# Softmax on one core: on exit Pool awaits the last stores, in place of SyncE

## The chip, the cores and the metric

One of the cores of a Trainium2 chip. The metric is device microseconds of one execution.

## The reference

```python
x = randn(16, 1024, 512), float32
x_max = np.max(x, axis=-1, keepdims=True)
exp_x = np.exp(x - x_max)
return exp_x / np.sum(exp_x, axis=-1, keepdims=True)
```

16384 rows of 512 elements: 33.6 MB in, 33.6 MB out.

## The kernel before

Loads are issued by SyncE (SP), stores by ScalarE (ACT). The framework ends a program with a block in which SyncE waits until every semaphore has its final value, all engines meet at a barrier that Pool (GpSimd) runs, Pool clears the semaphores, and a second barrier follows. The kernel edits that block when the program is complete, and has already merged the two barriers into one:

```python
def one_barrier_on_exit(nc):
    end = nc.main_func.blocks[2].instructions
    def of(engine, kind):
        return [i for i in end if i.engine == engine and type(i).__name__ == kind]
    for engine in (Activation, PE, DVE, SP):         # names shortened, an assertion cut
        arrivals = [i for i in of(engine, "InstDrain") if i.has_update()]
        leaves = of(engine, "InstEventSemaphore")
        end.remove(leaves[0])
        end.remove(arrivals[1])
    gather, release, gather_2, release_2 = of(Pool, "InstEventSemaphore")
    end.remove(release)
    end.remove(gather_2)
```

What is left in the exit block, engine by engine, as the built program has it (the compiler splits a drain's list of awaited semaphores into instructions of at most two semaphores, and leaves one with the drain):

```
SP    wait: store queue 3
SP    wait: store queues 4 and 2
SP    wait: store queues 5 and 1
SP    wait: queue 6 (the LAST store) and queue 0
SP    wait: queue 7 and VectorE's count
SP    drain, waits for ScalarE's count            } the moved drain
SP    drain, arrives at the barrier               (ACT, PE, DVE: likewise)
Pool  drain
Pool  gather: waits for four arrivals
Pool  drain ("reset drain"), clear of the semaphores, drain, release
all   leave when released
```

The first drain of the list is the "moved drain" of this document, Pool's wait for the four arrivals is the "gather", and the way from SyncE's arrival to Pool's gather is the "hop".

Of the kernel before, what the change touches and what calls it, by code (L numbers as in the profile page):

```python
# [1 line left out]

# [4 lines left out]

F32 = mybir.dt.float32
EXP = mybir.ActivationFunctionType.Exp
AX = mybir.AxisListType.X  # L10


CHUNKS = [
    (3, 0), (5, 3), (8, 8), (16, 16), (16, 32), (16, 48), (16, 64), (16, 80), (16, 0), (16, 16),
]
SBUF_ROWS = 96

EARLY = 8
AFTER_STORE = {2: [8], 3: [9]}

GROUP = 8

FINISH_BEFORE = (1, 2, 3)

STORE_ROWS = {3: 8, 4: 8, 5: 8}

ON_ACT = ()

AT_HEAD = {mybir.EngineType.SP: 3}



def loads_at_the_head(nc):

    main, body = nc.main_func.blocks[0], nc.main_func.blocks[1]
    for engine, count in AT_HEAD.items():
        loads = [
            i
            for i in body.instructions
            if i.engine == engine and type(i).__name__ == "InstDMACopy"  # L40
        ][:count]
        barrier = next(
            n
            for n, i in enumerate(main.instructions)
            if i.engine == engine and type(i).__name__ == "InstDrain"
        )
        for load in loads:
            body.instructions.remove(load)
        main.instructions[barrier:barrier] = loads
# [10 lines that stand above are left out]
    for engine in (  # L60
        mybir.EngineType.Activation,
        mybir.EngineType.PE,
        mybir.EngineType.DVE,
        mybir.EngineType.SP,
    ):
        arrivals = [i for i in of(engine, "InstDrain") if i.has_update()]
        leaves = of(engine, "InstEventSemaphore")
        assert len(arrivals) == len(leaves) == 2
        end.remove(leaves[0])
        end.remove(arrivals[1])  # L70
    gather, release, gather_2, release_2 = of(mybir.EngineType.Pool, "InstEventSemaphore")
    end.remove(release)
    end.remove(gather_2)

@with_exitstack
def kernel(
    ctx: ExitStack,
    tc: tile.TileContext,
    x: bass.AP,
    out: bass.AP,  # L80
):
    nc = tc.nc
    nc.at_finalize(loads_at_the_head)
    nc.at_finalize(one_barrier_on_exit)
    P = nc.NUM_PARTITIONS

    x_flat = x.flatten_outer_dims()
    out_flat = out.flatten_outer_dims()
    n, d = x_flat.shape
    assert n == P * sum(R for R, _ in CHUNKS)  # L90


    src, dst, at = [], [], 0
    for R, _ in CHUNKS:
        for flat, views in ((x_flat, src), (out_flat, dst)):
            part = flat[at : at + P * R, :]
            views.append(part.rearrange("(p r) d -> p r d", r=R))
        at += P * R

    data = ctx.enter_context(tc.tile_pool(name="data", bufs=1))  # L100
    stats = ctx.enter_context(tc.tile_pool(name="stats", bufs=4))
    held = data.tile([P, SBUF_ROWS, d], F32, name="held")
    place = [held[:, s : s + R, :] for R, s in CHUNKS]


    groups = []
    for k, (R, _) in enumerate(CHUNKS):
        m = -(-R // GROUP)
        cuts = [R * i // m for i in range(m + 1)]
        since = 0  # L110
        for a, b in zip(cuts, cuts[1:]):
            ends = b == R or b - since >= STORE_ROWS.get(k, R)
            groups.append((k, a, b, since if ends else None))
            since = b if ends else since
    shift = [None] * len(groups)
    sums = [None] * len(groups)

    def load(k):
        queue = nc.scalar if k in ON_ACT else nc.sync
        queue.dma_start(out=place[k], in_=src[k])  # L120

    def rowmax(g):
        k, a, b, _ = groups[g]
        shift[g] = stats.tile([P, b - a], F32, name="shift", tag="shift")
        nc.vector.reduce_max(  # L125
            out=shift[g], in_=place[k][:, a:b, :], axis=AX, negate=True
        )

    def exps(g):
        k, a, b, _ = groups[g]  # L130
        sums[g] = stats.tile([P, b - a], F32, name="sums", tag="sums")
        for r in range(a, b):
            nc.scalar.activation(  # L133
                out=place[k][:, r, :],
                in_=place[k][:, r, :],
                func=EXP,
                bias=shift[g][:, r - a : r - a + 1],
                scale=1.0,
                accum_out=sums[g][:, r - a : r - a + 1],
            )  # L140

    def scale(g):
        k, a, b, since = groups[g]
        recip = stats.tile([P, b - a], F32, name="recip", tag="recip")
        nc.vector.reciprocal(out=recip, in_=sums[g])  # L145
        for r in range(a, b):
            nc.vector.tensor_scalar_mul(  # L147
                out=place[k][:, r, :],
                in0=place[k][:, r, :],
                scalar1=recip[:, r - a : r - a + 1],  # L150
            )
        if since is not None:
            nc.scalar.dma_start(
                out=dst[k][:, since:b, :], in_=place[k][:, since:b, :]
            )
        if b == CHUNKS[k][0]:
            for later in AFTER_STORE.get(k, ()):
                load(later)

    with tc.manual_schedule():  # L160
        for k in range(EARLY):
            load(k)
        waiting = None
        for g, (k, a, _, _) in enumerate(groups):
            if waiting is not None and a == 0 and k in FINISH_BEFORE:
                scale(waiting)
                waiting = None
            rowmax(g)
            exps(g)
            if waiting is not None:  # L170
                scale(waiting)
            waiting = g
        scale(waiting)


# [1 line left out]
_INS = ['x']  # L177
_OUTS = [((16, 1024, 512), 'float32')]


# [23 lines left out]
```

## Time and profile before

| | before |
|---|---|
| median of the first three runs | 161.48 us (161.41 to 161.56) |
| span of the profiled run | 159.586 us |
| last store: issued, 16th increment of its semaphore | 144.932 us, 158.883 us |
| that landing to the end of the span | 703 ns |
| end of the span to the last semaphore update of the execution | 1941 ns |

The lines that carry this are in the prediction. Read the table as a sum of three terms: the landing (the moment of the 16th increment, 158.883 us), the handshake (from there to the end of the span, 703 ns), and the close (from there to the last semaphore update, 1941 ns). The measured time is a little less than the sum: this execution took 161.41 us, and the sum is 161.527. In all 13 profiles the time lies 0.105 to 0.120 us below the sum; why is not shown, but it is nearly constant, so a change of the sum shows in the time.

### The profile page before, as it was taken

What the parts mean: (1) busy time and instruction counts of PE and PEld (TensorE: products, weight loads), DVE (VectorE), ACT (ScalarE), POOL (GpSimd) and SP (SyncE); (2) the same over time, 40 slices, a digit from 0 to 9 for tenths busy, and PEclk for the clock granted to TensorE, in tenths of its full rate; (3) what the DMA queues carried; (4) which work ended last, traced back from release to release, by engine and by line L of the source; (5) the groups of instructions that cost most, each with busy time, mean ns of one, the idle gap of its engine ahead of it and who ended that gap; (6) DMA issues with size and microseconds to landing.
All of it is one profiled execution on the core that took longest, in us unless ns stands there. A gap on an engine that the chain in (4) does not pass through costs nothing.

```text
span 159.6 us, 511 instructions
## 1 busy us (share of the span) xinstructions
DVE 123.9 (78%) x162; ACT 93.3 (58%) x257; POOL 0.2 (0%) x4
## 2 busy tenths in 40 slices
DVE  0482880799699999999999999999999999853000
ACT  0717119207994959595958687776868595940000
POOL 0000000000000000000000000000000000000000
DMA  7999999899999999999899999999999999999993
GB/s 267 443 456 432 399 414 466 375 404 467 411 446 411 485 419 396 439 411 493 378 448 439 411 497 411 405 444 402 435 444 485 411 402 468 435 402 419 485 411 164
DMA packets 3315, 67.13 MB, mean 421 GB/s; under 512 B 368, under 2 KB 368, under 8 KB 624
## 3 DMA queue, kind: packets, MB, share of 16 engines
q1 hardware_dynamic: 1440, 33.56, 49.4%
q10 hardware_dynamic: 1872, 33.56, 49.0%
q14 instruction: 3, 0.02, 0.0%
HBM read 33.55 MB, written 33.55 MB: 421 GB/s over the span
## 4 chain that ended last, share of the span: by engine, by line
DVE 71%; ACT 14%; issue 3%; DMA 3%; DVEq 0%; ACTq 0%
DVE shift L125 39%; DVE held L147 30%; ACT held L133 14%; DMA held<-in_x_dram 3%; DVE recip L145 2%; DVEq L199 0%; ACTq L133 0%
## 5 line engine op out<-in xcount | busy, mean ns | idle before, releaser
L133 ACT ACTIVATE held<-held,shift 128x512 f32<-128x512 f32 x128 | 90.5, 708 | 43.4 <-DVE shift L125 33.3
L125 DVE TENSOR_REDUCE shift<-held 128x8 f32<-128x4096 f32 (+2 forms) x17 | 70.7, 4164 | 4.6 <-DMA held<-in_x_dram 4.6
L147 DVE TENSOR_SCALAR held<-held,recip 128x512 f32<-128x512 f32 x128 | 52.2, 482 | 0.6
L133 ACT ACTIVATION_READ_ACCUMULATOR held<-held,shift 128x1 f32 x128 | 23.9, 187 | 0.0
L145 DVE RECIPROCAL recip<-sums 128x8 f32<-128x8 f32 (+2 forms) x17 | 3.3, 195 | 15.8 <-ACT held L133 15.8
L133 ACT ACT_TABLE_LOAD x1 | 1.3, 1283 | 4.7 <-DMA held<-in_x_dram 4.7
L188 POOL MEMSET const-bfloat16-1.0<- 128x1 bf16 x1 | 0.1, 103 | 0.0
L188 POOL MEMSET const-uint8-127<- 128x1 uint8 x1 | 0.1, 102 | 0.0
L188 POOL MEMSET const-float32-1.0<- 128x1 f32 x1 | 0.1, 100 | 0.0
L188 POOL MEMSET const-float32-0.0<- 128x1 f32 x1 | 0.1, 99 | 0.2 <-issue 0.2
## 6 DMA issues: line engine op xcount, KB each, us to landing
held<-in_x_dram SPq DMA_DIRECT2D x7, 4096.0 KB, 41.8
out_dram<-held ACTq DMA_DIRECT2D x4, 4096.0 KB, 20.9
out_dram<-held ACTq DMA_DIRECT2D x7, 2048.0 KB, 35.3
held<-in_x_dram SPq DMA_DIRECT2D x1, 2048.0 KB, 11.7
held<-in_x_dram SPq DMA_DIRECT2D x1, 1280.0 KB, 7.2
out_dram<-held ACTq DMA_DIRECT2D x1, 1280.0 KB, 19.9
held<-in_x_dram SPq DMA_DIRECT2D x1, 768.0 KB, 4.6
out_dram<-held ACTq DMA_DIRECT2D x1, 768.0 KB, 15.6
```

The source lines that it names most:

```text
L125: nc.vector.reduce_max(out=shift[g], in_=place[k][:, a:b, :], axis=AX, negate=True)
L133: nc.scalar.activation(out=place[k][:, r, :], in_=place[k][:, r, :], func=EXP, bias=shift[g][:, r - a : r - a + 1], scale=1.0, accum_out=s ...
L145: nc.vector.reciprocal(out=recip, in_=sums[g])
L147: nc.vector.tensor_scalar_mul(out=place[k][:, r, :], in0=place[k][:, r, :], scalar1=recip[:, r - a : r - a + 1],)
L188: nc = _bacc.Bacc("TRN2", target_bir_lowering=False, num_devices=1)
```

## The change

The intent: SyncE waits for the stores and then only tells Pool so. If Pool waits itself, SyncE's arrival is early and the hop from one engine to the other leaves the end of the execution.

```diff
     end.remove(release)
     end.remove(gather_2)
+
+    done = of(mybir.EngineType.SP, "InstDrain")[0]
+    end.remove(done)
+    at = next(n for n, i in enumerate(end) if i.name == gather.name)
+    end.insert(
+        at,
+        mybir.InstDrain(
+            name=done.name, engine=mybir.EngineType.Pool,
+            ins=[], outs=[], sync_info=done.sync_info,
+        ),
+    )
```

More of the change, by code (lines that the diff above doesn't have):

```diff
@@ L73, in one_barrier_on_exit @@
     end.remove(gather_2)
+    done = of(mybir.EngineType.SP, "InstDrain")[0]
[4 more added lines that the diff above has]
+        mybir.InstDrain(
+            name=done.name,
+            engine=mybir.EngineType.Pool,
+            ins=[],
+            outs=[],
+            sync_info=done.sync_info,
+        ),
+    )
 @with_exitstack
```

## The prediction

> **What bounds the kernel now.** I read the page first, then cut the last 15 us into stretches, then asked the waits of SyncE's queue, then the instructions of the exit line in the last 0.8 us, and last the trace's records there one by one, because the page counts no drain or semaphore instruction as busy.
>
> From the page, the busy time of the engines, the DMA share over 40 slices of 4 us, and the two data queues (loads on q1, stores on q10):
>
> ```profile
> DVE 123.9 (78%) x162; ACT 93.3 (58%) x257; POOL 0.2 (0%) x4
> ...
> DMA  7999999899999999999899999999999999999993
> ...
> q1 hardware_dynamic: 1440, 33.56, 49.4%
> q10 hardware_dynamic: 1872, 33.56, 49.0%
> ```
>
> DMA is at 80% or more from the second slice to the last but one, and the two queues together fill 98.4% of the 16 engines' span. So transfers are the bound: 67.13 MB at the page's mean of 421 GB/s are 159.5 us of a 159.6 us span. GpSimd (Pool) does four memsets at the start and nothing else.
>
> The end, in stretches (columns: length, busy us of DVE, ACT and POOL with counts, clock, DMA share, GB/s):
>
> ```profile
> 145.00:150.00 5.00, 0.00 (x0) 0.00 (x0) 0.00 (x0) 1.00 1.00 433
> 150.00:155.00 5.00, 0.00 (x0) 0.00 (x0) 0.00 (x0) 1.00 1.08 465
> 155.00:159.60 4.60, 0.00 (x0) 0.00 (x0) 0.00 (x0) 1.00 0.43 185
> ```
>
> No engine computes after 145 us; the end is set by the stores draining, and after them by whatever handshake follows. The page's chain stops at the last VectorE multiply and says nothing of this end. The waits of SyncE's queue do:
>
> ```profile
> SPq L199 <- DMA out_dram<-held: 76.0, 4, 47.1
> SPq L199 <- PEq L199: 0.5, 1, 0.5
> ```
>
> SyncE has nothing left to issue after 82.8 us and sits in exit waits for stores (76.0 us in all), then 0.5 us for its own release. That release is put down to PE only because PE counts the same semaphore down; Pool raises it. The instructions of the exit line between 158.8 us and the end (count: shortest/median/longest ns, first and last start):
>
> ```profile
> L199 SPq EVENT_SEMAPHORE  x3: 17/27/28, 158.9 to 159.5; - x3
> L199 SPq DRAIN  x2: 7/7/7, 159.0 to 159.1; - x2
> L199 POOLq EVENT_SEMAPHORE  x2: 17/17/17, 159.1 to 159.5; - x2
> L199 POOLq DRAIN  x2: 34/52/70, 159.2 to 159.4; - x2
> L199 POOLq EVENT_SEMAPHORE_RANGE_CLEAR  x1: 93/93/93, 159.3 to 159.3; - x1
> ```
>
> All of it lies within 0.69 us. A drain takes 7 ns on SyncE, but 34 and 70 ns on Pool. The single records (start in ns, duration, instruction):
>
> ```
> 158883      -  the last store's semaphore gets its 16th increment
> 158900     27  SyncE waits: last store, and one older store
> 158961     28  SyncE waits: another store queue, and VectorE's count
> 159026      7  SyncE drain: ScalarE's count          <- moves to Pool
> 159085      7  SyncE drain: arrives at the barrier   <- stays on SyncE
> 159117     17  Pool waits for four arrivals
> 159198     70  Pool drain
> 159297     93  Pool clears the semaphores
> 159419     34  Pool drain
> 159482     17  Pool releases; the others leave at 159524 to 159535
> 159586         end of the span
> ```
>
> **What the Trainium skill says.** "Perfetto Trace Analysis", section "Sequencer-only Instruction (DRAIN, etc)", says that the profiler reports only the execution of such an instruction, not its wait nor the time for its update to spread. The trace agrees: SyncE's 7 ns drain is followed 59 ns later by the next instruction, so spacings have to be counted, not durations. "VectorE: DVE Perf Modes", section "The DRAIN you can't avoid", has boilerplate drains at about 12 ns on all five engines. For Pool this trace disagrees (34 and 70 ns here, 181 ns behind the memsets at the start), and the measurement decides. "DMA: Bandwidth & Descriptors", section "Why a DMA increments its semaphore by 16 and not by 1", says that the engines of one transfer finish independently and only the full 16 means landed. Here the 16 increments of the last store spread from 157.686 to 158.883 us, and SyncE moves on 17 ns after the sixteenth. "Runtime: NRT & Kernel Launch", section "The ~15µs preamble/postamble breakdown", has a barrier, a semaphore reset and more behind a kernel. The trace shows semaphore updates until 161.53 us, 1.9 us past the span, which accounts for 161.48 against 159.6. The change touches none of it.
>
> **The change, part by part.** It takes SyncE's first exit drain with its list of awaited semaphores and puts it on Pool, just before Pool waits for the four arrivals. In the built program the list becomes five semaphore instructions and the drain, in the old order, with the last store in the fourth of them. SyncE's arrival stays, but now comes at about 83 us instead of 159.085. Nothing in the loop, the loads or the stores moves. The order of instructions on each engine is otherwise the same but for line numbers.
>
> Removed from the path: SyncE's drain to its arrival, 59 ns, and the arrival to Pool's wake, 159117 - 159085 = 32 ns. Together 91 ns.
>
> Added to the path: Pool must run the same three instructions, then a fourth of its own, where it was standing ready before. Steps from the landing:
> - Landing to first wait passed: 17 ns on SyncE; no Pool wake from a DMA is in the trace, so I keep 17. Start at 158900.
> - First wait to second: 61 ns on SyncE (158900 to 158961). Pool's only two back-to-back semaphore instructions, in the entry barrier, are 78 ns apart (1525 to 1603), the first with an update that these lack. 61 to 78.
> - Second wait to drain: 65 ns on SyncE; on Pool 81 both at entry (1603 to 1684) and at exit (159117 to 159198), again with updates. 65 to 81.
> - Drain to the wait for arrivals: Pool's two exit drains lead to the next instruction after 99 ns (70 ns long) and 63 ns (34 ns long), so 29 ns plus the drain. 63 to 99.
>
> Sum 189 to 258 ns, so Pool's wait for arrivals would start at 159089 to 159158 against 159117 now. The arrivals are in by then (SyncE 83 us, VectorE and ScalarE by 145.5 us), so it passes at once. From there on all is the same. The change is worth between -28 ns and +41 ns; the middle is +7 ns, which is nothing: 0.004% of 161.48.
>
> **Rivals.** (1) The handshake disappears for its full 91 ns. It would need Pool to be as quick as SyncE, with a 7 ns drain, and a free final wait; 161.39 us. Against it are the two Pool drains above and the fact that the arrivals' wait still has to be executed. (2) Pool's drain is slow, as the 181 ns one behind the memsets, or Pool wakes slowly from a DMA's semaphore: 29 + 181 = 210 ns instead of 63 to 99 gives 161.6. Against it: that drain had memsets in flight, while at exit Pool has been idle for 158 us, and the drain at 1684 took 41 ns. (3) SyncE, freed at 83 us, lets something start earlier. But its last load is issued by then in both kernels, and ScalarE issues all stores, so there is nothing to start; no gain. (4) The whole exit handshake, 158883 to 159586 or 0.70 us, were saved: not on offer, and even that would be only 0.4%. Nothing in the trace carries this past 2%.
>
> **Range and chances.** The effect is smaller than the scatter of the three runs (161.41 to 161.56), so the prediction is the old median, 161.48. The range has to hold run scatter of 0.15 us, a possible different chip or session, which the trace does not tell, and rivals 1 and 2 (161.39 and 161.6). I take 161.25 to 161.70. A change of 2% would be 3.2 us, 4.6 times the whole handshake, so within 2% has 0.985; the rest is for what I do not see.
>
> **What would show it right or wrong.** In the changed profile the exit's store waits should appear on Pool's queue, SyncE's one wait there should be some 76 us for its release, and DMA rows and queue shares should be the same to 0.2 points. From the sixteenth increment of the last store to the end of the span it was 703 ns; I expect 675 to 744 ns. The moved drain should last 34 to 70 ns; 7 ns would speak for rival 1, over 150 ns for rival 2. I would be wrong if the landing-to-end interval changed by over 100 ns, or if the last store itself landed at another time by more than the scatter, which would mean that an idle Pool or SyncE queue touches the transfers.

## The result, and the profile after

The changed kernel took 161.53 us (median of 6 runs, 161.43 to 161.63), the kernel before 161.47 us (6 runs, 161.41 to 161.65). The ratio is 1.0002, with a 95% interval of 0.9989 to 1.0014: the same. Ratios here are the mean time of one kernel's fast runs over that of the other's of the same rounds, so not quite the ratio of the medians quoted.

Busy times and data queues of the page, changed kernel:

```profile
DVE 123.9 (78%) x162; ACT 93.3 (58%) x257; POOL 0.2 (0%) x4
...
q1 hardware_dynamic: 1440, 33.56, 49.5%
q10 hardware_dynamic: 1872, 33.56, 48.9%
```

The last stretches, changed kernel (length, busy DVE, ACT, POOL, clock, DMA share, GB/s):

```profile
145.00:150.00 5.00, 0.00 (x0) 0.00 (x0) 0.00 (x0) 1.00 0.99 426
150.00:155.00 5.00, 0.00 (x0) 0.00 (x0) 0.00 (x0) 1.00 1.05 452
155.00:159.81 4.81, 0.00 (x0) 0.00 (x0) 0.00 (x0) 1.00 0.46 198
```

Work and transfers are those of before: queue shares moved by 0.1 points, and the same bytes drain at the end. What moved is the wait. SyncE's own queue, changed kernel, first line of its waits:

```profile
SPq L214 <- PEq L214: 76.5, 1, 76.5
```

The 76.0 us of store waits are gone from SyncE; it now waits once for its release (again put down to PE, which counts the same semaphore down). The store waits are on Pool, under a line of the library, because the compiler made them from an instruction that carries no line of the kernel:

```profile
bacc.py:44 POOLq EVENT_SEMAPHORE  x5: 17/43/43, 130.1 to 159.2; - x5
```

And the exit line from 158.8 us on, changed kernel (shortest/median/longest ns, first and last start):

```profile
L214 POOLq EVENT_SEMAPHORE  x2: 17/17/17, 159.3 to 159.7; - x2
L214 POOLq DRAIN  x2: 34/52/70, 159.4 to 159.6; - x2
L214 POOLq EVENT_SEMAPHORE_RANGE_CLEAR  x1: 92/92/92, 159.5 to 159.5; - x1
L214 SPq EVENT_SEMAPHORE  x1: 17/17/17, 159.7 to 159.7; - x1
```

Two things are to be seen. A wait instruction for two semaphores takes 43 ns on Pool (median of the five), against 27 and 28 ns on SyncE before. And only two Pool drains are recorded where three ran: the moved one has no source line at all and is left out, which is why the page counts 510 instructions and before 511. Record by record, with the time since the landing:

```
ns after the landing of the last store       before          changed
wait: last store, queue 0                    SP    17        Pool  24
wait: queue 7, VectorE                       SP    78        Pool 111
drain: ScalarE                               SP   143        Pool (not recorded)
arrival                                      SP   202        (early)
Pool's gather                                     234             276
reset drain                                       315             357
clear                                             414             456
last drain                                        536             578
release                                           599             641
end of the span                                   703             745
```

From gather to end it is 469 ns in both. Ahead of it the changed kernel needs 276 ns where the old one needed 234: the hop is gone with the step to it, and what came in its place costs 42 ns more.

The landing itself was at 159.061 us in this profile and at 158.883 us before, 178 ns later, which is most of the difference of the two spans. Whether the change did that had to be tested.

### The profile page after: what moved, and what is told of

Its sections match the earlier page's. It is cut to its first block, busy times and chain, and to the rows that moved or that the text cites. A ratio compares the mean times of both kernels' runs of the same rounds, so it can differ in the third digit from the quotient of the medians.

```text
span 159.8 us, 510 instructions
## 1 busy us (share of the span) xinstructions
DVE 123.9 (78%) x162; ACT 93.3 (58%) x257; POOL 0.2 (0%) x4
## 4 chain that ended last, share of the span: by engine, by line
DVE 70%; ACT 14%; issue 3%; DMA 3%; DVEq 0%; ACTq 0%
DVE shift L140 38%; DVE held L162 30%; ACT held L148 14%; DMA held<-in_x_dram 3%; DVE recip L160 2%; DVEq L214 0%; ACTq L148 0%
```

## The experiments

**The theory:** every sequencer instruction behind the last landing is on the path with its start-to-start spacing, and these spacings are longer on Pool than on SyncE; that gives back the hop. **The rivals:** the waiting engine moves the landing; the handshake is absorbed by what follows the kernel; Pool's drain alone is to blame; Pool wakes slowly.

All edits stand behind the two removals at the end of `one_barrier_on_exit` of the kernel before. `made(...)` only builds an instruction and gives it the source line of `gather`, so that it is recorded. `waits` is the list of the SyncE drain `done`, `place_of(...)` finds an instruction's place in the block, `Event` is a semaphore instruction and `Drain` a drain. The diffs are cut to the lines that make the difference. "Spacing" is the time from the start of one instruction to the start of the next on its engine.

### The changed kernel with its drain made visible

```diff
+    end.remove(done)
+    end.insert(place_of(gather), made(Drain, done.name, POOL, waits))
```

> The changed kernel with only a source line given to the moved drain, so that the trace records it. My theory (Pool runs the same wait instructions more slowly, and that gives the saved hop back): from the landing of the last store's 16th increment to the end of the span 745 ns, within 10 of the first profile of the changed kernel (before: 703); Pool's wait starts 24 ns after the landing, the next 87 ns later, the drain 80 to 90 ns after that, lasts 34 to 70 ns, and the wait for arrivals follows after 75 to 85 ns. Rival (the 178 ns later landing in the first profile of the changed kernel is caused by Pool waiting in place of SyncE): the last store lands near 159.06 us again and the times lie 0.1 to 0.2 us above before in all rounds. My theory: the times of both kernels share the same range, 161.4 to 161.65.

Measured: 161.54 us (5 runs, 161.44 to 161.72; before 161.46, ratio 1.0007, interval 0.9995 to 1.0020). Landing to end 745 ns again. The exit line from 158.8 us on:

```profile
L215 POOLq EVENT_SEMAPHORE  x4: 17/30/43, 159.1 to 159.7; - x4
L215 POOLq DRAIN  x3: 34/34/70, 159.2 to 159.6; - x3
```

Now three drains are there. By records: wait at 24 ns after the landing, next wait 86 later, drain 87 later, lasting 34 ns, gather 78 later. These intervals are as the theory had them; the times are not quite (it had put both kernels at 161.4 to 161.65; the runs reach from 161.44 to 161.72, and from 161.32 to 161.59 before). The landing was at 159.053 us, which the rival of the moved landing had asked for too; the other runs have to decide that.

### Ten more satisfied waits, on Pool and on SyncE

```diff
+    old = [w for w in waits if w.ant_name.startswith(("DMAHW0", "DMAHW1"))]
+    for k in range(10):                       # Pool version, in the changed kernel
+        end.insert(place_of(gather), made(Event, f"I-{9000 + k}", POOL, old))
```

```diff
+    for k in range(10):                       # SyncE version, in the kernel before
+        end.insert(place_of(done) + 1, made(Event, f"I-{9000 + k}", SP, old))
```

> The changed kernel with ten more semaphore instructions on Pool behind the store waits, each of two semaphores long satisfied. My theory (each instruction behind the landing adds its spacing to the end, about 87 ns on Pool): landing to end 745 + 870 = 1615 ns, time 162.3 to 162.5. Rival (the handshake lies beside the close of the execution and is absorbed): landing to end longer in the trace, but time still 161.4 to 161.7.

> The kernel before with the same ten semaphore instructions on SyncE, between its store waits and its arrival. My theory: 61 ns each on SyncE, landing to end 703 + 610 = 1313 ns, time 162.0 to 162.2, so 26 ns less for each instruction than on Pool. Rival (the two engines are alike and the 42 ns are something else, such as a Pool wake or the drain): the ten cost the same on both, within 5 ns each.

Measured on Pool: 162.34 us (4 runs; ratio to before 1.0055, 1.0042 to 1.0069), landing to end 1612 ns. On SyncE: 162.09 us (4 runs; 1.0040, 1.0025 to 1.0056), landing to end 1313 ns. Exit line from 158.8 us on, Pool version, then SyncE version:

```profile
L218 POOLq EVENT_SEMAPHORE  x14: 17/43/43, 158.9 to 160.4; - x14
L218 POOLq DRAIN  x3: 34/34/70, 159.1 to 160.3; - x3
```

```profile
L216 SPq EVENT_SEMAPHORE  x13: 17/28/28, 159.0 to 160.2; - x13
L216 SPq DRAIN  x2: 7/7/7, 159.1 to 159.8; - x2
```

The same instruction, with semaphores that had long been satisfied, lasts 43 ns on Pool and 28 on SyncE. The ten add 867 ns on Pool (1612 - 745) and 610 ns on SyncE (1313 - 703), 26 ns more each on Pool. The times follow: the means lie 0.88 and 0.64 us above those of the kernel before, against 0.91 and 0.61 us in the trace. So nothing behind the kernel absorbs the handshake; that rival falls.

The Pool version holds one more finding. The compiler merged waits so that the first of the ten had one semaphore and the gather got two. The one with a single semaphore is followed by the next after 60 ns, all others after 86 or 87; the gather with two is followed by the reset drain after 107 ns, and with one after 80 or 81 in the other profiles in which the reset drain follows it directly. By these two comparisons the second semaphore of a wait costs 26 or 27 ns on Pool. Other pairs give somewhat less: 25 in the next experiment, and 20 or 21 in the two profiles of the reset version below, where a wait for one semaphore is followed after 66 ns.

### No drain among Pool's waits

```diff
-    end.insert(place_of(gather), made(Drain, done.name, POOL, waits))
+    end.insert(place_of(gather), made(Event, done.name, POOL, waits))
```

> The changed kernel with the moved drain replaced by a semaphore instruction; the waits are paired anew, with the last store in the third of five, so that as many instructions follow it as in the changed kernel. My theory (the number of Pool instructions counts, not that one is a drain): landing to end 735 to 765 ns, against 745. Rival (the Pool drain is the culprit): 40 ns or more shorter than 745.

The removed line is that of the version with the visible drain. Measured in one run of unknown state (161.52 us): landing to end 780 ns. That is 35 ns longer than with the drain, outside the 735 to 765 of my theory, and far from the rival's 705. By records, three spacings of 86, 87 and 87 ns lead from the first wait to the gather, and the gather, which got a second semaphore in the new pairing, is followed after 106 ns where it was 81. So nearly all of the excess is 25 ns for that second semaphore and 9 for a two-semaphore wait (87) in the drain's place (78). The moved drain is not what makes the changed kernel 42 ns longer: it is the cheapest of the three moved steps. But this run is no test of drain against wait alone, since the new wait has two semaphores and the drain had one. Where both have one, the drain is the dearer: it is followed after 78 or 79 ns, the wait after 60 (66 in the reset version).

### The last store awaited last, on SyncE and on Pool

```diff
+    waits.sort(key=lambda w: not w.ant_name.startswith("DMAHW6"))
+    end[place_of(done)] = made(Drain, done.name, SP, waits)          # SyncE version
```

```diff
+    waits.sort(key=lambda w: not w.ant_name.startswith("DMAHW6"))
+    end.remove(done)                                                 # Pool version
+    end.insert(place_of(gather), made(Drain, done.name, POOL, waits))
```

> The kernel before with SyncE's list of waits in another order: the last store is now awaited last, in the drain. My theory (every instruction behind the landing is on the path; two SyncE instructions, 61 + 65 ns, move ahead of it): landing to end 703 - 126 = 577 ns, and about 0.13 us less time. Rival (the order of satisfied waits costs nothing): 703 ns.

> The changed kernel with the same new order, on Pool. My theory: 745 less 87 and less about 85 ns, so 565 to 585 ns from landing to end; the move to Pool is then worth nothing either way against the SyncE version with that order (577). Rival (the move itself pays once the order is right): 91 ns below the SyncE version.

Measured on SyncE: landing to end 576 ns; 161.32 us (5 runs, 161.24 to 161.46) against 161.42 before; ratio 0.9992 (0.9980 to 1.0005). On Pool: 572 ns; 161.37 us (161.31 to 161.49); 0.9996 (0.9984 to 1.0009). Exit line from 158.8 us on, SyncE version:

```profile
L215 SPq DRAIN  x2: 7/7/7, 158.9 to 159.0; - x2
L215 POOLq EVENT_SEMAPHORE  x2: 17/17/17, 159.0 to 159.4; - x2
```

No SyncE wait instruction is left behind the landing, only its two drains. With the order right, the hop and the step to it cost 59 + 32 = 91 ns on SyncE and its replacement 8 (slower wake, 24 against 16) + 79 ns on Pool, and the two versions differ by 4 ns in the trace. Their times do not differ beyond their intervals. Moving the wait costs 42 ns in the old order and saves 4 in the new one; ordering it is worth 127 ns on SyncE (703 - 576) and 173 on Pool (745 - 572).

### One instruction fewer on each engine

```diff
+    end.remove(done)                              # SyncE's arrival waits for the last store
+    arrive = of(SP, "InstDrain")[0]
+    waits += arrive.sync_info.on_wait
+    end[place_of(arrive)] = made(Drain, arrive.name, SP, waits, arrive.sync_info.on_update)
```

```diff
+    end.remove(done)                              # Pool gathers first, its reset drain waits
+    reset = of(POOL, "InstDrain")[1]
+    end[place_of(reset)] = made(Drain, reset.name, POOL, waits, is_reset_sema=True,
+        reset_range_start=reset.reset_range_start, reset_range_stop=reset.reset_range_stop)
```

Both use the list with the last store last. The clear still stands behind every wait on what it clears, and all outputs were right.

> The kernel before with the last store awaited by SyncE's arrival drain itself, one SyncE instruction fewer behind the landing. My theory: 577 - 59 = 518 ns from landing to end. If the hop from SyncE to Pool cost much more than the 32 ns read off the trace, this would still be 100 ns or more above the version in which Pool's reset drain waits for more than the gather alone explains.

> Pool gathers the arrivals first, which are early, and its drain ahead of the clear waits for the last store: nothing but the fixed close of 388 ns (that drain's start to the end of the span, 159418 to 159806 in the changed kernel) is left behind the landing, plus a wake of 24 ns. My theory: 412 ns from landing to end, 0.29 us (0.18%) less time than before, the fastest of all. Rival (a drain that waits wakes more slowly, or the drain still takes its time after an idle Pool): 450 ns or more.

Measured, arrival version: 518 ns; 161.23 us (5 runs, 161.19 to 161.36; ratio 0.9988, 0.9976 to 1.0001). Reset version: 412 ns; 161.22 us, with runs from 161.09 to 161.72 (ratio 0.9993, 0.9980 to 1.0007). Both intervals inside the trace are to the nanosecond what the sum of spacings gave. So the wait on Pool does pay once the gather goes ahead of it: 106 ns less than the better SyncE version, because the hop (32 ns) and the gather (81 ns) are off the path and only the slower wake (7 ns) is added. In time, the 0.29 us and "the fastest of all" were not shown by these rounds. The reset version's 161.72 spoils its mean; that run had a span of 159.9 us where the other four had 159.3 to 159.5, and it left no trace.

### The changed kernel and both versions once more, on one chip

No edit; the three kernels as they were.

> The changed kernel once more, unaltered, beside the two best versions on one chip. My theory: landing to end 745 ns again, within 3; the landing itself anywhere between 158.85 and 159.07 us, as in the ten profiles so far; times 161.4 to 161.75, above the kernel before by 0 to 0.1 us. Rival (the engine that waits moves the landing): the landing at 159.05 or later, as in two of the earlier profiles with the waits in this order on Pool.

> The kernel in which SyncE's arrival drain waits for the last store, once more. My theory: landing to end 518 ns within 3, time about 0.18 us below before. Rival (the earlier gain came from the landing's scatter): no lower than before.

> The kernel in which Pool's reset drain waits for the last store, once more, since one of its five runs read 161.72. My theory: landing to end 412 ns within 3, time about 0.29 us below before and 0.1 below the arrival version; the single high run was a late landing and need not come again. Rival (this version has a second, slower state of its own): again a run at 161.6 or more, or a mean no lower than that of the arrival version.

Measured: the changed kernel 745 ns, landing at 158.948 us, 161.53 us (161.44 to 161.62; ratio to before 1.0004, 0.9991 to 1.0016). The arrival version 519 ns, 161.25 us (161.21 to 161.33; 0.9986, 0.9973 to 1.0000). The reset version 412 ns, 161.10 us (161.07 to 161.22; 0.9979, 0.9966 to 0.9991); before 161.43 us (9 runs, 161.37 to 161.71). The exit line of the reset version from 158.8 us on:

```profile
L225 POOLq DRAIN  x2: 34/52/70, 158.9 to 159.1; - x2
L225 POOLq EVENT_SEMAPHORE_RANGE_CLEAR  x1: 93/93/93, 159.0 to 159.0; - x1
L225 POOLq EVENT_SEMAPHORE  x1: 17/17/17, 159.2 to 159.2; - x1
L225 SPq EVENT_SEMAPHORE  x1: 17/17/17, 159.2 to 159.2; - x1
```

Behind the landing only the reset drain, the clear, the last drain and the release are left. The high run did not come again, and the kernel before had one like it in these rounds (161.71, span also 159.9), so it is no state of that version alone; what makes such a run is open. This version beats both kernels, by 0.2 to 0.3% (161.12 us in the mean against 161.48 before and 161.53 changed), clear of noise in these rounds and not in those of the first attempt.

**Did the waiting engine move the landing?** With Pool waiting, eight profiles have the last landing between 158.850 and 159.061 us, mean 158.951. With SyncE waiting, five have it between 158.883 and 159.017, mean 158.940. The means differ by 11 ns and the ranges overlap nearly whole. The 178 ns between the first two profiles are within this scatter: with Pool waiting in the old order alone, the landing fell anywhere from 158.886 to 159.061, and in the repeat of the changed kernel at 158.948, against the rival's 159.05 or later. A shift of a few tens of ns is too small for so few profiles and stays open. What causes the scatter, no run here shows.

## Why the prediction was right

The predicted 161.48 us, the range of 161.25 to 161.70 and "within 2%" hold: 161.53 us. That alone says little of the mechanism: 2% is 4.6 times the whole handshake, and the range also held rivals 1 and 2. The sharper test is the sum of steps behind the landing, and there the prediction had the mechanism right (the hop goes, slower Pool instructions take its place) and several sizes wrong. By its steps:

- **The bound.** Right. The transfers set the end, and the exit adds a fixed sum behind the landing. In all profiles the close is 1.940 to 1.946 us, so the time is landing + handshake + close less a constant (0.105 to 0.120 us), and only the handshake answers to such edits.
- **Removed, 91 ns.** Right: the spacings of 59 and 32 ns come again in the version with the reordered wait on SyncE, and leaving out one of the two instructions took 58 (576 - 518).
- **Added, each of its four terms.** The wake was taken as SyncE's 17 ns; it is 24 or 25 on Pool in every profile in which Pool waits for the last store. Wait to wait was put at 61 to 78; it is 86 or 87. Wait to drain was put at 65 to 81; it is 87. Drain to gather was put at 63 to 99; it is 78, with a drain of 34 ns. The two wait terms were read off unlike instructions. Those carried an update and awaited one semaphore or none; these have no update and await two. By the runs above a wait for one semaphore without an update has a spacing of 60 or 66, an update adds some 15 to 20 (the gather has 80 or 81), and a second semaphore 20 to 27: two errors of opposite sign, of which the second was larger. The last term lies in its range by luck. Its rule, "29 ns plus the drain", gives 63 for the drain of 34 ns that was measured; the next instruction came 44 ns behind that drain, and only the upper end, meant for a drain of 70 ns, covers the 78.
- **The sum.** I had -28 to +41 ns, middle +7; it is +42 ns in all three profiles of the changed kernel. So the expected landing-to-end interval of 675 to 744 ns missed by 1 ns, at its slow edge: the wake and both waits lie 6 to 9 ns above the upper ends used in the sum, and the drain 21 below its own. That the miss is so small is luck. In time the 42 ns are under the scatter of single runs. Over all rounds the mean of 16 runs of the changed kernel (the visible-drain version included) is 161.54 us and that of 33 runs of the kernel before 161.48, which are 0.065 us apart with a standard error of 0.027 us; runs on several chips are mixed in that, so it agrees with 42 ns and does not prove it. What it leaves for a shift of the landing is 0.02 us, within the error.
- **A sign of being wrong.** The prediction named a landing that moves by more than the scatter, which it had put at 0.15 us. The first profile showed 178 ns, so this sign appeared; over all profiles the landing scattered by 211 ns with Pool waiting (eight) and by 134 ns with SyncE (five), so 178 ns is no sign by itself, and the prediction's scatter was put too narrow.
- **The rivals.** The full 91 ns would have needed Pool to be as quick as SyncE and its last wait to be free; shown wrong. A slow wake (7 ns more) or a slow drain (34 ns) are no large terms; shown. That the freed SyncE starts nothing earlier is shown by the unchanged queues. The whole handshake was said to be "not on offer"; that was too hasty. Of its 703 ns, the reset version saved 291.

Where the expected gain of the change went: the hop and the step to it were on the path for 91 ns (59 + 32). In their place came the step from the moved drain to the gather, 78 ns, for Pool's gather, which stood ready before, now comes behind everything that was moved. So the removal itself gained 13 ns. Against them stand the two waits, which take 87 ns each on Pool and took 61 and 65 on SyncE (48 more), and the wake (7 more): 48 + 7 - 13 = 42 ns.

## What to carry to other kernels

In these runs the exit was a sum. Behind the last landing, count sequencer instructions by their start-to-start spacing, not by engine hops: an awaited semaphore that comes last belongs in the last wait, and everything that can be satisfied early (other waits, the gather of arrivals) ahead of it; here that was worth 127 to 291 ns. Moving a wait to another engine paid here only where fewer instructions were left behind the landing (106 ns in the reset version), not where the same ones ran on the slower engine (42 ns lost). With a transfer-bound kernel of 161 us all of this is worth at most a few tenths of a per cent, and a fixed interval inside the trace tells it where times scatter more.

## What the Trainium skill lacked or had wrong

- "VectorE: DVE Perf Modes", section "The DRAIN you can't avoid": it has the runtime's boilerplate drains at about 12 ns on all five engines. The prediction compared its Pool drains with this and called it a disagreement. That is not like with like: the drains recorded here carry the program's own lines, and the trace keeps no instruction without a line, so none of the runtime's is seen. What the page lacks is a figure for the program's entry and exit drains: here SyncE's at the exit take 7 ns, and Pool's 34 ns (the moved and the last one) and 70 ns (the one ahead of the clear, in every profile).
- "Perfetto Trace Analysis", section "Sequencer-only Instruction (DRAIN, etc)": right that wait and propagation are hidden, but without numbers. Here a two-semaphore wait without an update takes 59 to 67 ns to the next instruction on SyncE and 86 or 87 on Pool, a one-semaphore wait 60 or 66 on Pool, and a drain to the next instruction 52 or 59 on SyncE and, for a drain of 34 ns ahead of the gather, 78 or 79 on Pool.
- On no page that I read: the cost of the second semaphore in one wait, 20 to 27 ns on Pool (spacing; the records last 43 against 17 ns), with a record of 27 or 28 against 17 ns on SyncE; and the time from a store's 16th increment to the waiting instruction's start, 16 or 17 ns on SyncE, 24 or 25 on Pool.
- "Runtime: NRT & Kernel Launch", section "The ~15µs preamble/postamble breakdown": its three parts behind a kernel add up to some 5 us, an estimate from its figures (1.5, 1.5 and 2); the traces show semaphore updates until 1.94 us behind the span, in every profile; whether anything follows that leaves no update, they do not tell.
